# The transposes of the first differential head's values, moved behind the last sliding-window pair

## The chip, the cores and the metric

The kernel runs on one core of one Trainium2 chip. The metric is the device time of one launch in microseconds, as the median of several runs. One further execution was recorded by the hardware profiler; the profile and its trace are of that execution.

## What is computed

One decoder layer over 512 positions of width 1024, in float32. A normalised and modulated input goes through one wide input projection that feeds two token mixers: sliding-window attention with 8 heads, and differential attention with 4 heads. Cut to what matters here:

```python
proj = h @ w_in[l]
qa, ka, va, qd, kd, vd, ga, gd = jnp.split(proj, points, axis=-1)
out_a = _sliding_window_attention(qa, ka, va, sinks, slopes)      # window 128, softmax with a sink
# differential attention: two softmax maps per head
p = jax.nn.softmax(scores, axis=-1)
a = p[:, :, 0] - lam * p[:, :, 1]
out_d = rmsnorm(jnp.einsum('bhqs,bshe->bqhe', a, v), subln_g) * (1.0 - lam_init)
merged = sigmoid(ga) * (out_a @ w_branch_swa) + sigmoid(gd) * (out_d @ w_branch_diff)
x = x + gate1 * (merged @ w_out)
```

Then follow a second norm, a gated MLP with a short convolution, and a last norm. The modulation vectors (shift, scale, gate) come from `silu(c) @ w_ada`.

## The kernel before, in words

Every float32 matrix is split into a rounded high part and a low remainder (ScalarE casts, VectorE subtracts), and a product is three matmuls: high by high, high by low, low by high (`mm3`, line 121). TensorE's order is written out by hand. VectorE, ScalarE and the DMA queue on SP are ordered by a scheduler when the kernel is built, except in a few hand-ordered stretches; the scheduler's order depends on priorities, on named issue points and on the whole program, so an edit in one place can reorder neighbours.

The attention part weaves two kinds of work on TensorE. The first are *units*: projections of a head or a gate, eight contraction steps of three matmuls each, written as generators. `fill(n)` (line 539) emits n steps of the current unit and counts down the list `later`; `after(n, fn)` puts a function on that list to be run n steps later. The second are the attention steps, placed between the fills. Functions that have to wait for a place of their own are put in the lists of `beside` and run by `flush`.

The sliding-window part runs over four pairs of heads (line 932). For pair i: a fill, the scores of pair i+1 (line 587, tile `sw`), the transposes of pair i's first head (`swa_transpose`, line 646), a fill of two steps, the second head's transposes, a fill, the softmax of pair i+1, two more fills with the values of pair i between them for the first two pairs. For each head the transposes come in two blocks, `tp` of four and of three 128x128 transposes by TensorE (line 656), each into one bank of tag "t"; ScalarE copies the bank out (`pT`, line 658). There are two banks of tag "t". The probabilities that are transposed are exponentiated on ScalarE (line 635) and divided on VectorE (line 644).

Meanwhile the units of differential heads 0 and 1 fill the gaps: q, k and v of each head (`add_head`, line 678). The v unit leaves its result transposed (features by positions) in the bank `pw`; ScalarE copies it to `vT` (line 697). A function `turn` then transposes it back by four TensorE transposes into a bank of tag "t" (`pv`, line 702), from which ScalarE casts the high part and VectorE subtracts for the low part (lines 490 and 491, `evac`), both into the head's tile `qkv`. In the kernel before, `turn` is run `V_LAG` = 13 steps after the v unit; for head 0 that falls between the second head's transposes of the third pair and the first head's transposes of the fourth.

After the loop come the remaining units, then `flush("row")`: a product `pr` (line 873) that sums an accumulated row of the modulation over partitions, copied out by ScalarE (line 878, `row`) and stored by POOL's DMA (line 879). Then the values of pairs 2 and 3 (`oa`, line 666), and the differential part: scores `sd` (line 729), their masked maximum and reduction on VectorE (line 741), scaled maxima `dmx` (line 751), exponentials on ScalarE (line 761), the combination of both maps on VectorE (lines 764 to 766), transposes `td` (line 778) and the values `od` (line 789).

Beside all this VectorE accumulates the modulation rows: `arow` (lines 854 and 856) reads blocks `ra` of `w_ada`, each 512 KB, loaded on SP (line 832). These loads and the weight loads of the units (`w`, `wga`, `wba`; lines 521 and 896) share four buffers of tag "raw": a load is issued when an earlier block has been used up, by line 856 for a block of `ra` or by the subtraction of line 119 for weights. The blocks for one half row are called by their number here: ra_0, ra_2, ra_4 and ra_6; the first of the next half row is ra11_0.

Of the kernel before, what the change touches and what calls it, by code (L numbers as in the profile page):

```python
# [35 lines left out]
V_LAG = 13  # L36
# [18 lines left out]
def kernel(  # L55
# [38 lines left out]
    def fbank(name):  # L94
        return bank("f", 2, [P, S], name)
# [4 lines left out]
    def tbank(name, shape=(P, S)):  # L100
        return bank("t", 2, list(shape), name)
# [339 lines left out]
    for gi in range(KT):  # L441
        more = gi + 1 < KT
# [45 lines left out]
    def evac(hi, lo, src, scale=None):  # L488
        if scale is None:
            nc.scalar.copy(hi, src)  # L490
            nc.vector.tensor_sub(lo, src, hi.bitcast(F32))
        else:
            nc.scalar.activation(hi, src, AF.Copy, scale=scale)
            return nc.vector.scalar_tensor_tensor(lo, src, scale, hi.bitcast(F32), ALU.mult, ALU.subtract)
# [24 lines left out]
    def load_cols(src, col, name):  # L519
        r = raw_tile([P, KT, P], name)  # L520
        nc.sync.dma_start(r, src[:, col : col + P].rearrange("(a p) n -> p a n", p=P))
        return split_pair(r, [P, KT, P], name)
# [11 lines left out]
    def prefetch():  # L534
        while units and len(loaded) < 2:
            load, run = units.pop(0)
            loaded.append((load(), run))

    def fill(n):
        for _ in range(n):  # L540
            if not current:
                prefetch()
                if loaded:
                    wts, run = loaded.pop(0)
                    current.append(run(wts))
                    if tick[0]:
                        prefetch()
            if tick[0] == 7:
                prefetch()
            if current:  # L550
                try:
                    next(current[0])
                except StopIteration:
                    current.clear()
            for e in list(later):
                e[0] -= 1
                if e[0] <= 0:
                    later.remove(e)
                    e[1]()
            tick[0] += 1  # L560
            if tick[0] >= ADA_START and tick[0] % ADA_EVERY == 0:
                next(ada, None)

    beside = {"row": [], "sum": [], "norm": []}

    def after(n, fn):
        later.append([n, fn])

    def flush(*kinds):
        for kind in kinds:  # L570
            while beside[kind]:
                beside[kind].pop(0)()

    def steps(o, wts, rhs, nk, k0=0, cl=slice(0, P)):
        wh, wl = wts
        for k in range(nk):
            mm3(o, wh[:, k, cl], wl[:, k, cl], rhs[0][k0 + k], rhs[1][k0 + k], k == 0, k == nk - 1)
            if k < nk - 1:
                yield
# [7 lines left out]
    def swa_scores(i, blocks):  # L587
        if 0 in blocks:
            c = pairs[i] = Pair()
            c.mx, c.nm, c.lsum, c.es = (  # L590
                ap.tile([P, 2, NT], F32, tag=t, bufs=2, name=f"{t}{i}") for t in ("mx", "nm", "lsum", "es")
            )
            c.sb = [ap.tile([P, 2, P], F32, tag="st0", bufs=2, name=f"st{i}_0")]
            c.sb += [ap.tile([P, 2, 256], F32, tag="st", bufs=ST, name=f"st{i}_{n}") for n in range(1, NT)]
            c.pT = []
        c = pairs[i]
        sps = {
            (g, j): vbank(f"sw{i}_{g}_{j}").rearrange("p (a q) -> p a q", a=2)
            if len(blocks) == NT and (g, j) == (1, 1) else sbank(f"sw{i}_{g}_{j}", (P, 2, 256))
            for g in sorted({n // 2 for n in blocks}) for j in range(2)  # L600
        }
        for n in blocks:
            w = P if n == 0 else 2 * P
            k0 = max(0, n - 1) * P
            qs, ks = slice(n * P, (n + 1) * P), slice(k0, k0 + w)
            mm3_rows([
                (
                    sps[n // 2, j][:, n % 2, :w],
                    [qa[64 * j : 64 * j + 64, i, b, qs] for b in range(2)],
                    [ka[64 * j : 64 * j + 64, b, ks] for b in range(2)],  # L610
                )
                for j in range(2)
            ])
        for n in blocks:
            w = P if n == 0 else 2 * P
            if n == 2:
                c.first = c.last
            for j in range(2):
                with tc.high_priority(offset=HP):
                    c.last = nc.vector.tensor_tensor_reduce(  # L620
                        c.sb[n][:, j, :w], sps[n // 2, j][:, n % 2, :w], dsw[:, 256 - w : 256], 1.0, -3e38, ALU.add, ALU.max,
                        c.mx[:, j, n : n + 1],
                    )
# [22 lines left out]
    def swa_transpose(i, j):  # L646
        c = pairs[i]
        pt = ap.tile([P, 1024], F32, tag="aTh" if j == 0 else "aTl", bufs=2, name=f"pT{i}_{j}")
        c.pT.append(pt)
        for b in range(2):  # L650
            wb = 512 if b == 0 else 384
            tp = tbank(f"tp{i}_{j}_{b}")
            for m in range(wb // P):
                kb, n = 2 * b + m // 2, 2 * b + m // 2 + m % 2
                off = (kb - max(0, n - 1)) * P
                nc.tensor.transpose(tp[:, m * P : (m + 1) * P], c.sb[n][:, j, off : off + P], ident)
            with tc.high_priority(offset=HP):
                c.copied = nc.scalar.copy(pt[:, b * 512 : b * 512 + wb], tp[:, :wb])

    def swa_values(i):  # L660
        o = tbank(f"oa{i}") if i == 3 else vbank(f"oa{i}")
        for kb in (0, 2, 1, 3):
            w = P if kb == 3 else 2 * P
            for j in range(2):
                rows = slice(64 * j, 64 * j + 64)
                nc.tensor.matmul(
                    o[rows, kb * P : kb * P + w], va[:, kb, rows],
                    pairs[i].pT[j][:, kb * 256 : kb * 256 + w],
                    start=kb == 0, stop=kb == 3, tile_position=(0, 64 * j),
                )  # L670

        with tc.high_priority(offset=HP), tc.issue_after(pairs[3].divided.ins) if i == 2 else ExitStack():
            evac(outa[0][:, i], outa[1][:, i], o)
# [4 lines left out]
    def add_head(h):  # L678
        def q(wts):
            t = heads[h] = ap.tile([P, 6, S], F32R, tag="qkv", bufs=2, name=f"qkv{h}")  # L680
            o = fbank(f"pq{h}")
            yield from steps(o, wts, hT, KT)
            evac(t[:, 0], t[:, 1], o, 2.0 ** (2 * h - 1))

        def k(wts):
            t = heads[h]
            o = fbank(f"pk{h}")
            yield from steps(o, wts, hT, KT)
            evac(t[:, 2], t[:, 3], o)

        def v(wts):
            t = heads[h]
            o = fbank(f"pw{h}")
            yield from steps(o, wts, hT, KT)
            vT = ap.tile([P, S], F32, tag="tmp", bufs=2, name=f"vT{h}")
            with tc.high_priority(offset=HP):
                nc.scalar.copy(vT, o)

            def turn():
                pv = tbank(f"pv{h}")  # L700
                for m in range(NT):
                    nc.tensor.transpose(pv[:, m * P : (m + 1) * P], vT[:, m * P : (m + 1) * P], ident)
                evac(t[:, 4], t[:, 5], pv)

            after(V_LAG, turn)

        for run, col in ((q, COL_QD), (k, COL_KD), (v, COL_VD)):
            units.append((lambda col=col: load_cols(win, col + h * P, f"w{col}_{h}"), run))
# [223 lines left out]
    for i in range(SWA_PAIRS):  # L932
        more = i + 1 < SWA_PAIRS
        fill(SWA_FILL[3])
        if more:
            flush("row")
            swa_scores(i + 1, range(NT))
        swa_transpose(i, 0)
        fill(SWA_FILL[4])
        swa_transpose(i, 1)  # L940
        fill(SWA_FILL[5])
        if more:
            with tc.issue_after(pairs[i].copied.ins):
                swa_softmax(i + 1)
        fill(SWA_FILL[6])
        if i < 2:
            flush("row")
            swa_values(i)
        fill(SWA_FILL[7])
# [13 lines left out]
    for s in range(4 * DIFF_HEADS):  # L963
        h, n = divmod(s, NT)
# [971 lines left out]
```

## Time and profile before

| | us |
|---|---|
| median of 3 runs | 694.5 |
| lowest and highest of them | 694.41 and 695.66 |
| the profiled execution's own time | 695.87 |
| its span, from the first to the last instruction | 693.8 |
| its mean granted TensorE clock | 0.995 of full |

The profiled execution's time includes about 2.1 us around its span. In the lines of the profile, PE is TensorE's matmul side, PEld its weight loads, DVE is VectorE, ACT ScalarE, POOL GpSimd, SP SyncE. A timeline line gives start and duration in us, engine, source line, operation, result and operands, partitions by elements, count and, in brackets, the idle time before it and what ended it. A number in a line such as `x7` counts instructions merged into one entry. Consecutive matmuls overlap in these records, so what one costs is best read from start to start.

### The profile page before, as it was taken

To read this page: it belongs to the slowest core of one execution; us is meant where nothing else is said; L and a number is where in the kernel's file an instruction comes from. 1 tells how busy PE (TensorE), PEld (TensorE's weight loads), DVE (VectorE), ACT (ScalarE), POOL (GpSimd) and SP (SyncE) were. 2 spreads that over 40 slices of the span, in tenths; PEclk is the share of its full clock that TensorE was granted. 3 is DMA by queue.
4 is the path that set the end of the run, shared out by engine and by line. 5 is a ranking of instruction groups with operands and counts; after the bars stand their busy time and mean duration, and the time that the engine had idled before them with its cause. 6 is when DMAs were issued, how large, how long until landed. Compare 5 with 4: busy or idle time off the path is not lost. (4 is left out here: it accounts for less than half of the span.)

```text
span 693.8 us, 11248 instructions
## 1 busy us (share of the span) xinstructions
PE 681.7 (98%) x4203; PEld 594.1 (86%) x4203; DVE 565.4 (81%) x1073; ACT 383.7 (55%) x686; POOL 82.0 (12%) x100
## 2 busy tenths in 40 slices
PE   8999999999999999999999999999999999999995
PEld 5887777788888888888889999999999999888884
DVE  4999986887886566663689998888888999979997
ACT  6676674555552333332467756655565666656665
POOL 3000000000001000000030111111111102440300
PEclk9999999999999999999999999999999999999998
DMA  9985453453545766229726788776889647996903
GB/s 302 353 236 177 146 164 118 130 165 103 155 120 175 214 199 194 100 94 291 255 47 137 152 213 193 171 184 212 187 216 234 156 144 208 195 196 199 168 1 121
DMA packets 115926, 121.81 MB, mean 176 GB/s; under 512 B 4447, under 2 KB 93344, under 8 KB 115872
## 3 DMA queue, kind: packets, MB, share of 16 engines
q1 hardware_dynamic: 96958, 95.09, 43.0%
q0 software_dynamic: 18720, 25.73, 21.8%
q8 instruction: 33, 0.54, 0.3%
q10 hardware_dynamic: 194, 0.28, 0.1%
q14 instruction: 21, 0.17, 0.1%
HBM read 118.97 MB, written 2.11 MB: 175 GB/s over the span
## 5 line engine op out<-in xcount | busy, mean ns | idle before, releaser
L1265 PE MATMUL up<-t,m_whi 128*128 128x256 f32 x512 | 93.1, 283 | 0.0
L1265 PEld LDWEIGHTS up<-t,m_whi 128*128 128x128 f32 x512 | 79.9, 192 | 0.0
L1265 PE MATMUL up<-t,m_wlo 128*128 128x256 f32 x256 | 72.4, 283 | 0.0
L1265 PE MATMUL up<-bh,p_whi 128*128 128x256 f32 x232 | 65.7, 283 | 0.0
L1265 PE MATMUL up<-bl,p_whi 128*128 128x256 f32 x232 | 65.7, 283 | 0.0
L1265 PE MATMUL up<-bh,p_wlo 128*128 128x256 f32 x232 | 65.7, 283 | 0.0
L856 DVE SCALAR_TENSOR_TENSOR arow<-ra,cs,arow 128x512 f32<-128x512 f32 x56 | 42.0, 750 | 19.3 <-DMA ra<-in_w_ada_dram 18.5
L1265 PEld LDWEIGHTS up<-t,m_wlo 128*128 128x128 f32 x256 | 49.2, 192 | 0.0
L1265 PEld LDWEIGHTS up<-bh,p_whi 128*128 128x128 f32 x232 | 44.5, 192 | 0.0
L1265 PEld LDWEIGHTS up<-bl,p_whi 128*128 128x128 f32 x232 | 44.5, 192 | 0.0
L1265 PEld LDWEIGHTS up<-bh,p_wlo 128*128 128x128 f32 x232 | 44.5, 192 | 0.0
L1174 POOL DMA_DIRECT2D s<-in_w_up_dram x21 | 27.0, 1360 | 140.9 <-DMA s<-in_w_up_dram 83.5
L1202 ACT CAST m_whi<-s 128x1024 fp32r<-128x1024 f32 x31 | 32.5, 1048 | 11.1 <-DVE s L1196 6.3
L1206 DVE TENSOR_TENSOR m_wlo<-s,m_whi 128x1024 fp32r<-128x1024 f32 x31 | 37.8, 1220 | 0.0
L1265 PE MATMUL up<-t,p_whi 128*128 128x256 f32 x176 | 32.2, 283 | 0.0
L879 POOL DMA_DIRECT2D mod_rows<-row x8 | 4.9, 613 | 206.6 <-ACT row L878 206.6
L1265 PEld LDWEIGHTS up<-t,p_whi 128*128 128x128 f32 x176 | 27.5, 192 | 0.0
L1272 ACT ACTIVATE gT<-a,cv 128x512 f32<-128x512 f32 x22 | 17.7, 814 | 16.9 <-DVE a L1307 15.9
L185 POOL TENSOR_TENSOR r<-ms,mhalf 128x1 f32<-128x1 f32 (+1 forms) x16 | 12.6, 790 | 121.2 <-DVE ms L183 73.1
L1202 ACT CAST p_whi<-wa 128x1024 fp32r<-128x1024 f32 x18 | 18.7, 1042 | 12.6 <-PE up L1265 9.0
L761 ACT ACTIVATE sd<-sd,dmx 128x128 f32<-128x128 f32 (+3 forms) x32 | 17.6, 553 | 13.7 <-DVE dmx L751 13.7
L1206 DVE TENSOR_TENSOR p_wlo<-wa,p_whi 128x1024 fp32r<-128x1024 f32 x18 | 22.0, 1223 | 3.8 <-ACT p_whi L1202 3.8
(491 smaller groups left out, 2075.2 us busy)
## 6 DMA issues: line engine op xcount, KB each, us to landing
ra<-in_w_ada_dram SPq DMA_DIRECT2D x32, 512.0 KB, 3.9
wa<-in_w_up_dram SPq DMA_DIRECT2D x22, 512.0 KB, 4.0
s<-in_w_up_dram SPq DMA_DIRECT2D x21, 512.0 KB, 4.6
s<-in_w_up_dram POOLq DMA_DIRECT2D x21, 512.0 KB, 6.9
adaw<-in_w_ada_dram SPq DMA_DIRECT2D x12, 512.0 KB, 6.6
w<-in_w_in_dram SPq DMA_DIRECT2D x12, 512.0 KB, 4.6
a<-in_w_up_dram SPq DMA_DIRECT2D x11, 512.0 KB, 4.4
b<-in_w_down_dram SPq DMA_DIRECT2D x10, 512.0 KB, 4.7
```

Source lines behind the costliest of these rows:

```text
L185: nc.gpsimd.tensor_tensor(r0, ms, mhalf[:, :n], ALU.pow)
L761: exp = nc.scalar.activation(pm[m], pm[m], AF.Exp, bias=mx[:, m : m + 1], scale=slope, accum_out=ls)
L856: nc.vector.scalar_tensor_tensor(ac, r[:, a], cc, ac, ALU.mult, ALU.add)
L879: nc.gpsimd.dma_start(mod_rows[idx, hf * S : (hf + 1) * S].rearrange("(g n) -> g n", g=4), row[0:P:32])
L1174: nc.gpsimd.dma_start(dst, upblock(*blk), accum_op=ALU.add)
L1202: nc.scalar.copy(W[J, name][0], R[J, SRC[name]])
L1206: nc.vector.tensor_sub(lo, R[J, SRC[name]], hi.bitcast(F32))
L1265: nc.tensor.matmul(o[u], w[:, k, cu], b[:, k], start=name in ("p1", "m5", "p2") and k == 0 and x == 0, stop=k == 3 and x == 2, skip_group_ ...
L1272: nc.scalar.activation(grow(j), av[J][:, u], AF.Identity, bias=cv[:, 66 + j : 67 + j], scale=cv[:, 44 + j : 45 + j])
```

## The change

`turn` of head 0 is no longer counted down. It is put in a new list and flushed in the last round of the pair loop, after the second head's transposes of the last pair and the fill behind them. Heads 1 to 3 keep the lag.

```diff
-    beside = {"row": [], "sum": [], "norm": []}
+    beside = {"row": [], "sum": [], "norm": [], "turn": []}
...
                 evac(t[:, 4], t[:, 5], pv)
 
-            after(V_LAG, turn)
+            if h:
+                after(V_LAG, turn)
+            else:
+                beside["turn"].append(turn)
...
         swa_transpose(i, 1)
         fill(SWA_FILL[5])
+        if not more:
+            flush("turn")
         if more:
             with tc.issue_after(pairs[i].copied.ins):
                 swa_softmax(i + 1)
```

In the program as it is built, the four transposes stand behind the last step of head 1's v unit and ahead of `pr`. ScalarE's cast moves with them, from ahead of the cast of head 1's `pk` to behind the copy `vT` of head 1. On VectorE the scheduler's order differs in one stretch, from the subtraction of `pv` to the second block of transposed differential probabilities; on SP two loads have exchanged what they wait for. POOL's order is the same.

## The prediction, made before the result was known

> **What bounds the kernel now.** I read the page first: the busy shares, the clock line, then what TensorE waits for, longest first.
>
> ```profile
> span 693.8 us, 11248 instructions
> PE 681.7 (98%) x4203; PEld 594.1 (86%) x4203; DVE 565.4 (81%) x1073; ACT 383.7 (55%) x686; POOL 82.0 (12%) x100
> ```
>
> ```profile
> PE tp L656 <- DVE qkv L491: 2.1, 1, 2.1
> PE a L174 <- POOL ones L133: 1.0, 1, 1.0
> ```
>
> TensorE is busy in 681.7 of 693.8 us. Its two longest waits are shown (total us, times, longest); the second belongs to the start. The first stands out: a transpose of line 656 once waited 2.1 us for line 491 on VectorE. What TensorE saves should reach the end, unless a feeder falls behind. The timeline shows that wait:
>
> ```profile
> 101.84 1.08 DVE L644 TENSOR_SCALAR st<-st,lsum 128x128 f32<-128x128 f32 x4
> ...
> 102.89 0.60 PE L656 MATMUL tp<-ident,st 128*128 128x128 f32 x4
> ...
> 103.35 0.56 ACT L490 CAST qkv<-pv 128x512 fp32r<-128x512 f32 x1
> ...
> 103.81 0.58 ACT L490 CAST qkv<-pk 128x512 fp32r<-128x512 f32 x1
> 103.88 1.07 DVE L644 TENSOR_SCALAR st<-st,lsum 128x128 f32<-128x128 f32 x4
> 104.29 0.58 ACT L658 COPY pT<-tp 128x512 f32<-128x512 f32 x1
> 104.87 0.68 DVE L491 TENSOR_TENSOR qkv<-pv,qkv 128x512 fp32r<-128x512 f32 x1
> ...
> 105.61 0.55 PE L656 MATMUL tp<-ident,st 128*128 128x128 f32 x3 [2.12 <-DVE qkv L491]
> ...
> 105.92 0.48 PE L122 MATMUL pw<-hThA,w_h 128*128 128x512 f32 x1
> ...
> 108.33 1.59 PE L656 MATMUL tp<-ident,st 128*128 128x128 f32 x7
> ...
> 109.67 0.48 PE L122 MATMUL pw<-hThB,w_h 128*128 128x512 f32 x1
> ...
> 111.23 0.43 PE L873 MATMUL pr<-arow,ones 128*32 128x128 f32 x8
> ```
>
> Two banks of tag "t" serve all these transposes. Head 0's values (pv) took one at 96.96, but ScalarE and VectorE empty it only at 103.35 and 104.87, behind pair 3's exponentials and divisions. The fourth pair's second block (the three tp at 105.61) needs that bank. TensorE stands still from 103.49 to 105.61, and the clock then falls. In the view by windows the columns are stretch, its length, busy time and count of PE, PEld, DVE, ACT and POOL, then the granted clock and DMA:
>
> ```profile
> 105.00:106.00 1.00, 0.39 (x4) 0.39 (x5) 1.00 (x2) 0.00 (x0) 0.00 (x0) 1.00 0.00 0
> 106.00:107.00 1.00, 1.00 (x5) 0.81 (x4) 0.15 (x1) 0.48 (x1) 0.00 (x0) 0.63 0.00 0
> ...
> 109.00:110.00 1.00, 1.00 (x7) 0.96 (x6) 0.00 (x0) 0.53 (x2) 0.00 (x0) 0.66 0.00 0
> ```
>
> ```profile
> 10.00:100.00 90.00, 89.26 (x540) 72.77 (x541) 81.14 (x242) 62.13 (x148) 1.09 (x2) 1.00 0.74 228
> 110.00:689.00 579.00, 576.13 (x3616) 511.44 (x3614) 476.28 (x800) 309.25 (x510) 75.84 (x75) 1.00 0.64 167
> ```
>
> Half the clock for a part of the first and of the last gives means of 0.63 and 0.66, so the slow stretch runs from about 106.26 to 109.68: 3.4 us, in which 1.7 us of work is lost. Everywhere else up to 689 us the clock is full (1.00).
>
> **The change, part by part.** It moves three things for head 0 from among pair 2's transposes to behind pair 3's last projection step, in front of pr (line 873): four transposes, ScalarE's cast and VectorE's subtraction. No instruction and no DMA is added, and POOL's order stays. The prices on TensorE at full clock are read from the pair before:
>
> ```profile
> 94.03 0.48 PE L122 MATMUL pk<-hThA,w_h 128*128 128x512 f32 x1
> ...
> 95.49 0.93 PE L656 MATMUL tp<-ident,st 128*128 128x128 f32 x7
> ...
> 96.17 0.48 PE L122 MATMUL pk<-hThA,w_h 128*128 128x512 f32 x1
> ...
> 96.96 0.60 PE L702 MATMUL pv<-ident,vT 128*128 128x128 f32 x4
> ...
> 97.32 0.48 PE L122 MATMUL pk<-hThA,w_h 128*128 128x512 f32 x1
> ```
>
> Seven transposes take 0.68 us from start to start (95.49 to 96.17), six projection matmuls 1.46 (94.03 to 95.49), four pv transposes 0.36 (96.96 to 97.32). Taking pv out also spares the slow first matmul behind it; I take 0.45 earlier arrival. The new course:
> - First tp of pair 3: 102.89 - 0.45 = 102.44. Its first group needs the divisions that end at 102.92 (101.84 + 1.08), so the last two transposes come just in time: next pw at 103.17 (102.44 + 0.68 + 0.05).
> - Six matmuls: tp of the second head at 104.63. It needs divisions of 103.88 to 104.95, each about 0.27, which arrive one by one just ahead of it, and the first bank's copy, now 0.46 earlier because pv's cast no longer stands before it. Next pw 105.31, then pv at 106.77.
> - pv 0.36, and 0.07 for the change of shape: pr at 107.20 instead of 111.23. **Gain 4.03 us.** By parts: 2.33 (the three tp would have begun at about 103.28, not 105.61) and 1.61 of clock (105.92 to 109.67 takes 3.75, at full price 1.46 + 0.68 = 2.14), with pv's 0.4 us coming and going.
>
> No idle of over 0.1 us is left there, so I count the clock as full.
>
> What does the moved work now delay? On ScalarE the cast stands between vT and row. oa of pair 3 takes pr's bank and so waits for row. Behind pw's end at about 106.9 come vT and the cast, 0.6 each, and row: 108.3. oa of pair 2 keeps TensorE until 109.2 (107.20, plus the 0.36 from pr to oa, plus half of the 3.25 for both, in the next fence). That is 0.9 us of cover; past it each us would cost one. pv of head 1 takes the moved pv's bank, which VectorE empties at about 109, several us before that pv comes, behind a whole gate projection. Head 0's values are first read by od (line 789), behind head 0's last softmax, later than all of this.
>
> VectorE's queue is changed more than the text of the kernel tells, since its order is arranged anew up to about 132 us. Two things count. wga_l (line 119) goes behind the four score reductions; and line 856, which multiplies the ada rows and waits for their DMA, is put elsewhere: the pair on ra_4 is now in front of w_l and in front of sd_2's softmax. On SP the order stays, but ra_4's load waits for wga_l, and of the next two loads ra_6 now waits for w_l and ra11_0 for line 856, the reverse of before. These rows carry the estimates:
>
> ```profile
> 111.59 3.25 PE L666 MATMUL oa<-pT,va 128*64 128x256 f32 x32
> ...
> 111.73 0.49 DVE L854 TENSOR_SCALAR arow<-ra,cs 128x512 f32<-128x512 f32 x1 [5.57 <-PE pr L873]
> ...
> 116.70 1.22 DVE L119 TENSOR_TENSOR wga_l<-wga,wga_h 128x1024 fp32r<-128x1024 f32 x1
> ...
> 117.83 0.29 DVE L741 CUSTOM_DVE_ANT_0 sd<-sd,ddf 128x128 f32<-128x128 f32 x1
> ...
> 118.94 0.29 DVE L751 TENSOR_SCALAR dmx<-dmx 128x2 f32<-128x2 f32 x2
> ```
>
> ```profile
> 122.37 0.75 DVE L856 SCALAR_TENSOR_TENSOR arow<-ra,cs,arow 128x512 f32<-128x512 f32 x1 [1.17 <-DMA ra<-in_w_ada_dram]
> ...
> 124.22 0.68 DVE L491 TENSOR_TENSOR qkv<-pv,qkv 128x512 fp32r<-128x512 f32 x1
> 124.83 1.22 DVE L119 TENSOR_TENSOR w_l<-w,w_h 128x1024 fp32r<-128x1024 f32 x1
> ...
> 127.68 0.75 DVE L856 SCALAR_TENSOR_TENSOR arow<-ra,cs,arow 128x512 f32<-128x512 f32 x1 [0.49 <-DMA ra<-in_w_ada_dram]
> ...
> 131.90 0.62 DVE L766 SCALAR_TENSOR_TENSOR sd<-sd,dls,sd 128x384 f32<-128x384 f32 x1
> ```
>
> ```profile
> 124.96 0.44 PE L778 MATMUL td<-ident,sd 128*128 128x128 f32 x2 [0.17 <-DVE qkv L491]
> 132.79 0.49 PE L778 MATMUL td<-ident,sd 128*128 128x128 f32 x3
> ```
>
> ```profile
> DMA to landing us min/median/max: 3.6/3.9/5.3
> ```
>
> L854 waits for pr, so it begins at 107.7. From there to wga_l's end took 6.19 us (111.73 to 117.92); now pv's subtraction (0.6) and the reductions (117.83 to 118.94, 1.11, and 0.1 for one dmx) are added: 115.7. ra_4 is issued then and lands 3.9 us later, the median of the 32 ra loads: 119.6. VectorE is there by then: from dmx to the end of head 1's pv subtraction took 5.96 us (118.94 to 124.90) with a DMA wait of 1.17 and two line 856 of 0.7 in it, so about 3.4 without, 119.1. Behind line 856 (0.66) the stretch from w_l's start to sd_2's L766 took 7.07 us (124.83 to 131.90). It loses the 0.49 wait and gains one more line 856 (0.70) and two tiny operations (0.40): 7.68. So L766 ends at 119.6 + 0.66 + 7.68 + 0.62 = 128.6. The three td, at 132.79 before, can come 4.03 + 0.17 = 4.2 us sooner, since td_1's 0.17 wait goes too: 128.6. **It just fits**; allowing 0.2 for this last meeting, 4.0 remain. With the smallest landing the gain is 4.2; with the largest, 5.3, L766 ends at 130.0 and the gain is 2.8. Behind that point all engines have their old order and their old waits. By the same reckoning VectorE's and SP's releases there come 3 to 4 us earlier; the one that hardly moves, ra11_0's load, still lands before VectorE comes to it. So I cost the rest of the kernel at nothing: it is shifted whole.
>
> The sum: 4.0 us off the profiled execution's own 695.87 us (span 693.8, 2.1 around it) is 691.9. The three timed runs have their median at 694.5, 1.4 below that execution, so **690.5 us**.
>
> [...] The windows show half clock from 0.65 us after an idle stretch of 2.12 us. [...]
>
> **The rivals.**
> - *Only the wait goes; the slow clock has another cause and stays.* Gain 4.0 - 1.6 = 2.4: 692.1 us. For it: the clock falls only 0.65 us after work has begun again. Against: the clock is 1.00 in all the rest, and this stretch stands right behind the only wait over 1 us. Chance 0.08. [...]
> - *ra_4 lands as late as the slowest ra load.* Gain 2.8: 691.7. For: it has VectorE's whole softmax queued behind it, back to back. Against: the queue holds no other load close by. Chance 0.10.
> - *The wait is traded for one as long at td.* If ra_4 lands 6.4 us after issue, TensorE stands 2.5 us at td and the clock falls again for 1.6: 694.5, no change. Chance 0.06, with any way in which the move does nothing, such as another holder of the bank.
> - *Slower, by the same mechanism, from 6.4 us on.* Each further us costs one. The longest median landing on the page is 9.1 us:
>
> ```profile
> chain_outh<-in_w_down_dram POOLq DMA_DIRECT2D x6, 512.0 KB, 9.1
> ```
>
>   With that TensorE stands 5.2 at td and loses 1.6 more: 2.6 us slower, 697.1. To be slower by over 1.4 it takes 7.8. Against: that is POOL's queue late in the kernel, and no ra load took over 5.3. Chance 0.06.
>
> **How the numbers follow.** The forecast, gain 3.4 to 4.6, has 0.70. Below it lie the two weaker gains, 0.18 together. A measurement of this kernel can tell 0.2%, 1.4 us, from no change: faster 0.88, within 0.06, slower 0.06. The range goes from 689.9 (4.6: the smallest landing and 0.4 for the steps I rounded) to 692.3 (the clock rival, 0.2 around it), which leaves out about 0.15.
>
> **What would show it.** Right: no PE wait for line 491 at tp; granted clock 1.00 from 100 to 115 us; pr near 107.2; the three td near 128.7; every later stage about 4 us earlier. Wrong: a slow window still near 106 us (clock rival), or a PE wait at td for sd (L766), with line 856 waiting for ra in front of it on VectorE past 120 us. The forecast fails if ra_4's landing is over 5.3 us, or if the clock falls without a stall.

## The result, and the profile after

| | before | after |
|---|---|---|
| median, us | 695.65 (12 runs) | 693.09 (12 runs) |
| lowest and highest, us | 694.05 and 697.90 | 692.31 and 693.68 |
| profiled execution, us (its span) | 695.87 (693.8) | 693.06 (691.3) |
| its mean granted clock | 0.995 | 0.996 |

The ratio of after to before is 0.9963, with a 95% interval of 0.9952 to 0.9974: 2.6 us less, where 4.0 us less and 690.5 were forecast. Before itself has a median of 695.65 over these twelve runs; the three runs shown ahead of the prediction had 694.5.

Line numbers of after are three higher than those of before from line 705 on: 873 is 876, 778 is 781, 856 is 859, 764 to 766 are 767 to 769.

The page of after begins with its span and the busy shares, then the waits of TensorE at this place (total us, times, longest):

```profile
span 691.3 us, 11249 instructions
PE 680.5 (98%) x4203; PEld 592.7 (86%) x4203; DVE 565.3 (82%) x1073; ACT 384.6 (56%) x686; POOL 82.1 (12%) x100
```

```profile
PE tp L656 <- DVE st L644: 0.5, 1, 0.5
```

The wait of 2.1 us for line 491 is gone. In its place the transposes waited 0.5 us for the divisions of pair 3 themselves (line 644). The windows of after, with the columns as before, and the timeline:

```profile
105.00:106.00 1.00, 1.00 (x6) 0.79 (x5) 0.84 (x5) 1.00 (x4) 0.00 (x0) 1.00 0.34 129
106.00:107.00 1.00, 1.00 (x10) 0.89 (x8) 1.00 (x4) 0.44 (x3) 0.00 (x0) 1.00 0.00 0
109.00:110.00 1.00, 1.00 (x16) 0.59 (x18) 0.58 (x2) 1.00 (x4) 0.00 (x0) 1.00 0.00 0
100.00:115.00 15.00, 14.51 (x104) 11.01 (x104) 11.29 (x32) 10.73 (x30) 0.77 (x1) 1.00 0.41 119
```

```profile
96.32 0.93 PE L656 MATMUL tp<-ident,st 128*128 128x128 f32 x7
...
103.88 1.13 PE L656 MATMUL tp<-ident,st 128*128 128x128 f32 x7 [0.49 <-DVE st L644]
...
106.25 0.93 PE L656 MATMUL tp<-ident,st 128*128 128x128 f32 x7
...
108.39 0.60 PE L702 MATMUL pv<-ident,vT 128*128 128x128 f32 x4
...
108.92 0.43 PE L876 MATMUL pr<-arow,ones 128*32 128x128 f32 x8
...
130.35 0.52 PE L781 MATMUL td<-ident,sd 128*128 128x128 f32 x3
```

The clock stays at 1.00 from 100 to 115 us. Each block of seven transposes is now one group: nothing stands between the four and the three any more, and pv comes behind the second block. How much was gained is read from one instruction in both timelines. Pair 2's transposes, ahead of the change, stand at 95.49 in before and 96.32 here: this execution was 0.83 us late when it came to the change. pr stands at 111.23 and 108.92, the three td at 132.79 and 130.35, and the spans end 2.5 us apart. So 2.31 + 0.83 = 3.1 us were gained up to pr, 2.44 + 0.83 = 3.3 up to td, and about 3.3 at the end. The trace has the gain that was forecast but for 0.7 us; the medians have 1.4 us less than forecast. The experiments look for both differences.

### The profile page after: what moved, and what is told of

It is laid out like the page before. It is cut to its first block, busy times and chain, and to the rows that moved or that the text cites. A ratio compares the mean times of both kernels' runs of the same rounds, so it can differ in the third digit from the quotient of the medians.

```text
span 691.3 us, 11249 instructions
## 1 busy us (share of the span) xinstructions
PE 680.5 (98%) x4203; PEld 592.7 (86%) x4203; DVE 565.3 (82%) x1073; ACT 384.6 (56%) x686; POOL 82.1 (12%) x100
## 5 line engine op out<-in xcount | busy, mean ns | idle before, releaser
L1270 PE MATMUL up<-t,p_wlo 128*128 128x256 f32 x88 | 24.9, 283 | 0.0
```

The lines of the kernel that those rows point to most:

```text
L1270: nc.tensor.matmul(o[u], w[:, k, cu], b[:, k], start=name in ("p1", "m5", "p2") and k == 0 and x == 0, stop=k == 3 and x == 2, skip_group_ ...
```

## The experiments

Two theories went into the first four. **Theory A**: the slow clock follows the stall only in part of the executions, so its 1.6 us can't be taken off a median of runs that mostly lack it. **Theory B**, the rival: it follows each time, and the missing part is given back by VectorE's new order or by pair 3's divisions. They ran on one chip with the same runs of before beside them: median 696.44, 23 runs.

### Before, unchanged

> The kernel before, unchanged, timed against itself: the ratio should be 1 within 0.2%. What it is for is the single executions, each with its span and mean granted clock. [...] Theory B (the slow clock comes with the stall every time): every profile shows both, and the spread of the times is that of the loads at the start.

Measured: 695.97 us median, 11 runs from 694.27 to 698.63, ratio 0.9996 (0.9984 to 1.0008). Five executions had a mean clock of 0.997 and took 694.27 to 695.23 us; six had 0.993 to 0.995 and took 695.97 to 698.63. The profiled one (696.38 us) is of the second kind; its waits and its windows:

```profile
PE tp L656 <- DVE qkv L491: 2.6, 1, 2.6
```

```profile
106.00:107.00 1.00, 0.84 (x5) 0.77 (x6) 0.70 (x2) 0.26 (x1) 0.00 (x0) 1.00 0.00 0
107.00:108.00 1.00, 1.00 (x4) 0.79 (x3) 0.00 (x0) 0.22 (x1) 0.00 (x0) 0.65 0.00 0
108.00:109.00 1.00, 1.00 (x5) 0.76 (x4) 0.00 (x0) 0.00 (x0) 0.00 (x0) 0.50 0.06 16
109.00:110.00 1.00, 1.00 (x7) 1.00 (x6) 0.00 (x0) 0.39 (x1) 0.00 (x0) 0.50 0.00 0
110.00:111.00 1.00, 1.00 (x4) 0.81 (x4) 0.00 (x0) 0.68 (x2) 0.00 (x0) 0.64 0.00 0
```

The seventh number of a line, behind the five engines, is the granted clock. The half clock begins 1.1 us after work does and again lasts 3.4 us (0.70 + 1 + 1 + 0.72, from means of 0.65 and 0.64 for the outer two).

Over all executions of before recorded for the experiments, 73 of them, 51 had a mean clock of 0.993 to 0.995 and a median of 696.51 us; 22 had 0.996 to 0.998 and a median of 694.93. That is 1.6 us apart, as much as the slow stretch costs in the trace. Theory A holds: before has two kinds of executions. That the group with the lower clock is the one with the slow stretch is shown for the two profiled ones, both with 0.995; none of the other group was profiled. A mean clock doesn't tell where the clock fell: one execution of after (below) has 0.995 from a slow stretch at its start. But of the 78 executions of the kernels here in which this stall is gone or partly filled, that is the only one at 0.995 or less.

### Before, with the stall partly filled

Two dummy matmuls of 512 columns stand behind the four transposes, where TensorE waits. They write to a score bank that nobody reads. Nothing else moves on any engine.

```diff
                 nc.tensor.transpose(tp[:, m * P : (m + 1) * P], c.sb[n][:, j, off : off + P], ident)
+            if (i, j, b) == (3, 0, 0):
+                kw = sbank("kw").rearrange("p (a n) -> p a n", a=4)
+                for _ in range(2):
+                    nc.tensor.matmul(kw, ones, ones4, start=True, stop=True)
```

> The kernel before, with two idle 512-column matmuls (about 0.9 us each) put on TensorE into the stall, ahead of the three transposes that wait; their result is read by nobody. The stall stays as long as it was, but TensorE is busy in it. Theory B: no slow stretch, 1.6 us faster than before (ratio 0.9977). Theory A with the slow clock in a share p of the executions: 1.6 p faster, so 0.8 us (0.9988) for half of them. If the clock had another cause: no change, and the slow stretch is still there.

Measured: 695.10 us, 11 runs from 694.68 to 696.46, ratio 0.9980 (0.9972 to 0.9989); every mean clock 0.996 to 0.998. The waits, and the slow place in the windows:

```profile
PE tp L656 <- DVE qkv L491: 0.7, 1, 0.7
```

```profile
100.00:115.00 15.00, 14.35 (x99) 10.14 (x98) 9.52 (x23) 9.67 (x26) 0.77 (x1) 1.00 0.29 87
```

The bank is still late, since the transposes still wait for line 491, but TensorE stands for 0.7 us and the clock stays full. The time becomes that of before's executions without the slow stretch (694.93): the clock alone is worth 1.6 us where it falls. The median doesn't separate the two theories, since its interval holds the numbers of both (0.9977 and about 0.9984 for 51 of 73); the single executions of before do. The clock rival of the prediction, that the slow stretch has another cause than the stall, falls here.

### Before, with pv in another bank

```diff
-                pv = tbank(f"pv{h}")
+                pv = (tbank if h else sbank)(f"pv{h}")
```

The transposes of head 0's values stay where they were, and no engine's order changes. Only the bank is another, so that the fourth pair doesn't wait for it.

> The kernel before with head 0's four transposes where they were, but into a bank of tag s instead of tag t, so that the last pair's transposes do not wait for it. The order of instructions is the old one on every engine. Theory B, where the changed kernel loses part of its gain by VectorE's new order or by pair 3's softmax: 3.7 us faster than before (0.9947), more than the changed kernel's 2.6. Theory A: 2.1 us and the share of the clock, about 2.6 to 3 (0.996), like the changed kernel. If pair 3's divisions bind in place of the bank: about 3 us, with a wait of TensorE for line 644 at tp.

Measured: 692.48 us, 6 runs from 691.26 to 693.85, ratio 0.9943 (0.9930 to 0.9955). TensorE's timeline there; none of these entries has a wait:

```profile
96.62 0.93 PE L656 MATMUL tp<-ident,st 128*128 128x128 f32 x7
...
104.01 0.93 PE L656 MATMUL tp<-ident,st 128*128 128x128 f32 x7
106.18 0.98 PE L656 MATMUL tp<-ident,st 128*128 128x128 f32 x7
108.49 0.43 PE L873 MATMUL pr<-arow,ones 128*32 128x128 f32 x8
...
129.86 0.49 PE L778 MATMUL td<-ident,sd 128*128 128x128 f32 x3
```

Pair 2's transposes stand at 96.62 here, 1.13 us later than in before, and pr at 108.49, 2.74 earlier: 3.9 us gained, of the 3.94 that the wait and the clock are worth (2.33 and 1.61). At td it is 2.93 + 1.13 = 4.1. So the bank is the whole cause, and the gain is kept when nothing else moves. The ratio is the number of Theory B (0.9947) and not that of Theory A (0.996). But Theory B put it beside a smaller gain of the changed kernel, and that kernel has 0.9947 in these same runs (next): before's median is 0.8 us higher here than in the first comparison and after's 0.7 lower. Theory B's general form, that something behind gives it back in any case, falls.

### After, once more

> The changed kernel once more, on the same chip and against the same executions of before as the three others: a ratio of 0.9963 within 0.1%. Its profile shows whether the 0.5 us that TensorE waited at tp for line 644 come each time (theory: pair 3's divisions now bind) or came from one late load (theory: 0 to 0.2 us in an execution whose loads land as in the profile of before).

Measured: 692.39 us, 5 runs from 691.86 to 693.81, ratio 0.9947 (0.9935 to 0.9959). The expected 0.9963 within 0.1% was missed. Mean clocks are 0.996 to 0.998. The profiled one took 693.56, with these waits:

```profile
PE td L781 <- DVE dls L767: 1.6, 1, 1.6
...
PE tp L656 <- DVE st L644: 0.3, 1, 0.3
```

At tp the wait is 0.3 us here, so it is not 0.5 each time, nor below 0.2. The other wait was not there in the first profile of after: 1.6 us at the three td. On VectorE's timeline, just ahead of it:

```profile
120.41 0.75 DVE L859 SCALAR_TENSOR_TENSOR arow<-ra,cs,arow 128x512 f32<-128x512 f32 x1 [1.56 <-DMA ra<-in_w_ada_dram]
121.08 1.22 DVE L119 TENSOR_TENSOR w_l<-w,w_h 128x1024 fp32r<-128x1024 f32 x1
...
128.18 0.75 DVE L859 SCALAR_TENSOR_TENSOR arow<-ra,cs,arow 128x512 f32<-128x512 f32 x1 [1.78 <-DMA ra<-in_w_ada_dram]
128.84 0.16 DVE L767 RECIPROCAL dls<-dls 128x1 f32<-128x1 f32 x1
...
129.88 0.62 DVE L769 SCALAR_TENSOR_TENSOR sd<-sd,dls,sd 128x384 f32<-128x384 f32 x1
```

The first of these lines waits for ra_4, the second line 859 for ra_6. ra_6's load may start only when w_l has freed its buffer (122.3), and it landed at 128.18. VectorE's order is the same in all four profiles of after: sd_2's reciprocal and sum, which the three td need, stand behind line 859, and were late by the wait of 1.78. In the first profile of after the same line waited only 0.38 us, and the three td came 0.15 us after L769 had ended (0.14 here).

So a part of Theory B came back in a narrower form, and two further theories went into the next experiments. **Theory D**: ra_6 in front of sd_2's softmax is what TensorE meets at td, in some executions. **Rival E**: that softmax is late in itself, behind ra_4 and the score reductions. The next four ran together; before had 696.48 there, 22 runs.

### After, with the softmax ahead of the load

```diff
                 probs[s] = pm[0]
+                lasts[s] = last
...
-                hold = tc.high_priority(offset=HP // 2)
+                hold = tc.issue_after(lasts[2].ins) if (idx, hf, k) == (1, 0, 6) else tc.high_priority(offset=HP // 2)
```

Line 859 for ra_6 is held back until sd_2's softmax has been issued. In the built program VectorE's order changes in that one place; the other engines keep the order of after.

> The kernel after with one thing put elsewhere: on VectorE the three softmax instructions of the first head's third block (sd_2, lines 767 to 769) come ahead of the line that waits for the load ra_6, instead of behind it; every other engine keeps the order of after. Theory D (the load in front of that softmax is what TensorE meets at td, 0.2 us in one execution of after and 1.6 in another): no TensorE wait for VectorE at line 781, whatever the landing of ra_6, and 0.3 to 1.2 us less than after on the median. Rival E (the softmax chain is late in itself, since the ada row ra_4 and the score reductions stand ahead of it too): a wait of about the same size stays at line 781 and the median is that of after within 0.3 us.

Measured: 691.96 us, 5 runs from 691.76 to 692.06, ratio 0.9939 (0.9925 to 0.9953). VectorE and TensorE in its timeline (line 860 is 859 of after, 782 is 781):

```profile
125.07 0.74 DVE L860 SCALAR_TENSOR_TENSOR arow<-ra,cs,arow 128x512 f32<-128x512 f32 x1
...
126.92 0.62 DVE L769 SCALAR_TENSOR_TENSOR sd<-sd,dls,sd 128x384 f32<-128x384 f32 x1
127.55 0.72 DVE L860 SCALAR_TENSOR_TENSOR arow<-ra,cs,arow 128x512 f32<-128x512 f32 x1
...
129.08 0.49 PE L782 MATMUL td<-ident,sd 128*128 128x128 f32 x3
```

L769 now ends at 127.54, 1.5 us before the td that needs it, with ra_4's second line 860 still in front (125.07). Rival E would have kept it late. Against after beside it (next) the median is 1.6 us lower, more than the 0.3 to 1.2 expected. In both profiles of this kernel ra_6 landed early (3.9 and 4.3 us after issue), so that a late landing does no harm here is shown by the times alone.

### After, beside it

> The kernel after unchanged, beside the others on the same chip. Theory D: ratio to before 0.994 to 0.997, with a TensorE wait at line 781 of 0 to 1.6 us that goes with the landing of ra_6 (3.8 to 5.8 us after issue). Rival E: the wait at line 781 does not go with that landing.

Measured: 693.56 us, 11 runs from 691.65 to 696.08, ratio 0.9959 (0.9946 to 0.9972). Three runs lie at 691.65 to 692.07, seven at 693.08 to 693.97. The one at 696.08 was profiled, and it was late from the first 20 us on: TensorE waited 1.05 and 1.70 us at line 408 (0.8 together in before), and the granted clock then fell to half from 11.72 to 15.14 us. So its end is not compared; its later part shows the wait again:

```profile
PE td L781 <- DVE dls L767: 1.5, 1, 1.5
```

The landing of ra_6 by itself is seen where the DMA view is limited to the stretch in which only that load is issued; the last number is the time from issue to landing. First the first profile of after, then the kernel above with the softmax ahead, then this one:

```profile
ra<-in_w_ada_dram SPq DMA_DIRECT2D x1, 512.0 KB, 4.4
```

```profile
ra<-in_w_ada_dram SPq DMA_DIRECT2D x1, 512.0 KB, 3.9
```

```profile
ra<-in_w_ada_dram SPq DMA_DIRECT2D x1, 512.0 KB, 5.7
```

In the four profiles of after (one of them is shown further below) the landings are 3.8, 4.4, 5.7 and 5.8 us, and the waits at td none, none listed, 1.5 and 1.6 us. They go together, as Theory D has it. By the waits of line 859, VectorE comes to it 4.0 us after ra_6's issue (5.8 less 1.78, 5.7 less 1.73, 4.4 less 0.38), so every landing beyond that is waited for.

### The other bank, beside after

> The kernel before with pv of the first differential head in a score bank instead of a transpose bank, a second time beside after: no order changed, only the bank wait gone. Theory D (after pays 0.3 to 0.5 us at tp for pair 3's divisions and 0.2 to 1.6 at td, this kernel pays neither): 0.5 to 1.5 us less than after. Rival E (those small waits are taken up by slack further on): within 0.3 us of after.

Measured: 692.96 us, 5 runs from 691.96 to 693.26, ratio 0.9950 (0.9937 to 0.9964). It is 0.6 us below after here and was 0.1 above it the first time. The spread of both is larger than that, so this pair decides nothing between Theory D and Rival E. Nor is this kernel without small waits: its profile has 0.3 us at pv for the score bank and 0.3 at td for line 491.

### Before, with one dummy matmul

`range(2)` in the diff above becomes `range(1)`.

> The kernel before with one dummy matmul of 512 columns, instead of two, in the stall at tp: the stall is cut to between the 0.7 us with two dummies and the 2.1 to 2.6 us with none. [...] Rival (any stall above a fixed length of about 1 us makes the clock fall, and the share depends on something else): the share stays at two in three and the median at about 696.0.

Measured: 695.24 us, 11 runs from 694.51 to 696.99, ratio 0.9988 (0.9978 to 0.9998). The wait at tp is 1.7 us, and no execution has a mean clock below 0.997. So 1.7 us of standing still didn't bring the slow stretch once in 11, where the 2.1 and 2.6 us of before bring it in 51 of 73. Fewer such executions than in before, or none, is what Theory A has here if a shorter stall brings the slow clock less often, and none came; a fixed length somewhat above 1.7 us with another reason for the remaining third is not excluded by this run; the stretches of work shown with the last experiment speak against it.

### The two versions of after, again

Whether the narrow group of the reordered kernel was chance (**Rival F**) was asked last; before had 696.35 there, 17 runs. First the kernel with the softmax ahead:

> The kernel after with sd_2's softmax ahead of the load ra_6 on VectorE, a second time. Theory D: one narrow group of times near 692.0, with none of the executions of after that are 1.5 us longer; no TensorE wait at line 781. Rival F (the narrow group of the first time, five runs from 691.76 to 692.06, was chance): two groups 1.5 us apart as in after.

Measured: 691.88 us, 6 runs from 691.37 to 692.53, ratio 0.9942 (0.9930 to 0.9955). After beside it:

> The kernel after unchanged, beside the others on the same chip. Theory D: two groups of times, near 692.0 and near 693.6, the upper one with a wait of about 1.5 us at line 781; median 0.5 to 1.7 us above that of the kernel with the softmax moved ahead. Rival F: the same distribution as that kernel, medians within 0.3 us.

Measured: 692.09 us, 6 runs from 691.92 to 693.42, ratio 0.9948 (0.9935 to 0.9961). Five runs lie at 691.92 to 692.34 and one at 693.42; the medians differ by 0.2 us, which in these runs alone is Rival F's number. Taken together, the 22 runs of after in the three experiments have 11 from 691.65 to 692.39 (median 692.01) and 10 from 693.08 to 693.97, with the one at 696.08 above them; of 11 runs with the softmax ahead, none is above 692.53 (median 691.96). Theory D stands. How often the upper group comes differs from one experiment to the next: 2 of 5, 8 of 11 (with the one at 696.08), 1 of 6. This profile of after, one without the wait, shows the forecast's course nearly as it was written:

```profile
95.59 0.93 PE L656 MATMUL tp<-ident,st 128*128 128x128 f32 x7
...
107.70 0.43 PE L876 MATMUL pr<-arow,ones 128*32 128x128 f32 x8
...
129.01 0.49 PE L781 MATMUL td<-ident,sd 128*128 128x128 f32 x3
```

Pair 2's transposes are 0.10 us later than in before's profile, and pr, the three td and the end of the span are 3.53, 3.78 and 3.9 earlier. So from the one profile to the other the gain is 3.6, 3.9 and 4.0 us, the last being the forecast's gain.

### Before, with the bank held longer

```diff
                 evac(t[:, 4], t[:, 5], pv)
+                if h == 0:
+                    nc.vector.tensor_sub(t[:, 5], pv, t[:, 4])
```

> The kernel before with the subtraction of line 491 for pv of the first head done twice (the second gives the same values again), so that pv's bank comes free later: the second stands behind the subtraction of head 1's k, and the stall at tp grows by about 1.2 us, to between 3.2 and 3.8 us. [...] Rival (the share has nothing to do with the stall's length): a third of the executions keep a clock of 0.996 or more.

Measured: 694.61 us, 12 runs from 693.61 to 696.44, ratio 0.9986 (0.9974 to 0.9998). The edit didn't do what it was for. In its profile the transposes wait for another thing:

```profile
PE tp L656 <- ACT pT L658: 1.6, 1, 1.6
```

The banks were dealt out anew when the kernel was built: the three transposes now take the bank of an earlier tp, which ScalarE's copy frees, and wait 0.5 us less than in before, not 1.2 more. Four of the 12 executions have a mean clock of 0.994 or 0.995, three of them above 696 us. By its mean clocks, then, a kernel whose profiled wait is 1.6 us has the slow stretch now and then, and the one with 1.7 us (one dummy matmul at its start) hasn't. A longer stall was not obtained, and the length of the wait in one profile is not enough to tell.

The traces show what decides. In three profiles the clock falls twice, once in the middle or at the start, and once at the end of the kernel, where TensorE has run out of work: at 106.26 and 689.94 us in before's, at 107.30 and 690.98 in before's second, at 11.72 and 690.97 in the late one of after (read from means of single microseconds, such as 0.63 for 106 to 107). The two falls are 583.68, 583.68 and 679.25 us apart. Before's trace records its slow stretch as 3.413 us long, and the distances are 171.0, 171.0 and 199.0 times that. In all 13 traces the first rise of the clock, at 4.9 to 9.7 us, lies a whole number of such lengths ahead of the last fall as well (in before 200.0, from 7.28 us on; in the first profile of after 199.0, from 6.71 to 685.97), so stretches of this length, counted back from the last fall, lie differently against the start of the kernel from execution to execution. Counted so, the 13 profiles have 16 falls of the full clock, each behind a stretch with at most 1.59 us of TensorE's work; behind none with 1.70 us or more did it fall. Four such stretches, of before, its second profile, the late one of after and this kernel; behind the first three the clock fell, behind the fourth it didn't. TensorE's busy time is the second number:

```profile
102.85:106.26 3.41, 1.29 (x10) 0.96 (x9) 2.67 (x9) 2.08 (x8) 0.00 (x0) 1.00 0.25 96
103.89:107.30 3.41, 1.14 (x7) 1.01 (x8) 2.61 (x8) 2.00 (x6) 0.00 (x0) 1.00 0.11 43
8.31:11.72 3.41, 1.59 (x6) 0.73 (x6) 0.96 (x7) 2.44 (x5) 0.76 (x2) 1.00 1.11 327
102.77:106.18 3.41, 1.78 (x12) 1.42 (x11) 2.78 (x10) 2.64 (x8) 0.00 (x0) 1.00 0.29 111
```

With full work on both sides, a stall of 0.7 us leaves at least 2.7 us of work in every stretch of 3.413 us, and one of 1.7 us at least 1.7; one of 2.12 or 2.58 leaves 1.29 or 0.83 where it falls whole into one. If the clock falls behind stretches with at most 1.59 us of work, or with anything below 1.70, an estimate from these figures is 55 to 62% of the executions for a stall of 2.12 us and 69 to 75% for 2.58; before has 51 of 73, which is 70%. This agrees with Theory A. The 4 of 12 here weren't profiled; by the same estimate they need a stall of more than 1.7 us, which stays unshown.

## Why the prediction was right in its mechanism and wrong in its number

- **The bank wait.** Right. It was put at 2.33 us; it is gone in every profile of after, and another bank alone removes it.
- **The slow clock.** Right as a consequence of the stall (filling the stall removes it) and in size: 1.61 against 1.6 between the groups. No profile of after has a granted clock below 1.00 from 100 to 115 us. The forecast took it to come each time; by the mean clocks it came in 51 of 73 executions.
- **The step that failed: "The three timed runs have their median at 694.5, 1.4 below that execution, so 690.5 us."** It was treated as a constant offset. It was no offset: the profiled execution had the slow stretch, and by their times the runs at 694.41 and 694.5 lie with the 22 executions without it (median 694.93), below the lowest of the 51 with it (695.61, median 696.51). The clocks of those three runs are not on record. From such a base only the 2.4 us of the prediction's own clock rival can be saved, which gives 692.1; the 4.0 us belong to a base of 696.5, which gives 692.5. Executions of after without the wait at td have 692.0. The row that could have warned was on the table: 695.66 beside 694.41 and 694.5, with a term of 1.6 us in the sum that only the profiled execution was known to have.
- **"It just fits."** The second term that was mis-sized, 0.2 us for the meeting at td. In the profiles of after it is about 0.1 us in the first, nothing in one, 1.5 and 1.6 us in the others; in the times of the experiments' 22 runs the lower 11 have a median of 692.01 and the upper 11 of 693.62, 1.6 apart. (The 12 runs of the first comparison are spread from 692.31 to 693.68 without a gap.) The rival *ra_4 lands as late as the slowest ra load* had this place and nearly this price, with a chance of 0.10, but the wrong load. Its reason against, "the queue holds no other load close by", was the error: line 859 for ra_6 stands six instructions ahead of sd_2's sum, and the prediction itself had noted that its load now waits for w_l. It took off before's 0.49 us wait for that load instead of working the wait out anew; it measured 0.38, 1.78 and 1.73 us where the profile shows one. With VectorE there 4.0 us after the issue, the median landing of 3.9 just fits and the slowest of before's profile, 5.3, already costs 1.3.
- **The first tp.** "Just in time" cost 0.5, 0.3 and 0.3 us in three of the profiles, and nothing in the one with pr at 107.70. The forecast had pr at 107.20.
- **Everything behind is shifted whole.** Right: in the first profile of after TensorE's instructions come 2.5 us earlier than in before from 140 us to the end, so no later stage gives anything back.
- **Slower.** The slower rival, a landing of over 6.4 us, didn't come: ra_6's were 3.8 to 5.8. A wait of 1.6 us at td brought no slow stretch either: the mean clocks of after's upper group are 0.996 to 0.998 but for the one execution with the slow stretch at its start, and in the stretches of 3.413 us that hold the two profiled waits at td TensorE was busy for 0.63 and 0.55 of the time.

Of the miss of 2.6 us (693.09 - 690.5), 1.15 is the base of the same comparison (695.65 instead of 694.5), and the other 1.4 the gain. That the slow stretch is absent from part of before's runs, and the new wait present in part of after's, is shown by the experiments; how the 1.4 divide in that comparison isn't. Its one profile of after has 0.5 us at tp and 0.1 at td, and was 0.8 later than before's profile ahead of the change, for which there is no cause on record.

The kernel with the softmax ahead of the load is the better version: 691.96 and 691.88 us, the lowest median both times, 4.5 us below before. Its lead over after is 1.6 us the first time and 0.2 the second.

## What to carry to other kernels

A saving may be subtracted only from executions that pay it: when the profiled execution is slower than the timed ones and holds an episode (a slow clock, a late load), sum from the profile for that kind of execution, and sum again without the episode for the others. After a reordering, list every instruction that now stands in front of the one the bottleneck needs and waits for a DMA, and work out each one's issue anew from what frees its buffer; a wait read from the old order is no price. And where a wait is for a buffer, another buffer removes it without moving anything.

## What the runs showed of the hardware that was not expected

- The granted clock fell to half for 3.4 us after TensorE had stood 2.1 or 2.6 us (two profiles). By the mean clocks this happened in 51 of 73 executions of one unchanged program, in none of 22 with the stall at 0.7 or 1.7 us, and in 4 of 12 of a kernel with a profiled wait of 1.6 us. The two groups of before are 1.6 us apart.
- In the 13 profiles the 16 falls of the full clock lie whole multiples of 3.413 us, the slow stretch's length in before's trace, behind its first rise. In the last 3.413 us ahead of each of them TensorE had at most 1.59 us of work; behind no stretch counted so that held 1.70 us or more did the clock fall. Waits of 1.05 and 1.70 us with sparse work between them were enough at the start of one execution.
- One and the same 512 KB load, in the same place of the same program, landed 3.8, 4.4, 5.7 and 5.8 us after issue in four executions. What makes the difference wasn't tried.
